# Issuing layer A of a two-layer trunk in the source's order

## Chip, core and metric

The kernel runs on one core of one Trainium2 chip. The metric is the device time of one execution in microseconds (us); of several runs the median is given. The engines are named as in the profile: PE is TensorE (matrix products), ACT is ScalarE, DVE is VectorE, POOL is GpSimd, and SP is the engine that issues most of the transfers (DMAs).

## The reference

A trunk of two layers works on 256 tokens of width 2048. Layer A is a Mamba-2 mixer, layer B is sliding-window attention with 32 heads over 4 shared key/value heads. Each layer ends in a layer norm of `alpha * x + mixer(x)`. Cut to what matters:

```python
# layer A
zxbcdt = x @ w_in                      # 2048 -> z 4096, x 4096, B 1024, C 1024, dt 64
xbc = silu(causal_conv4(xbc) + conv_b)
dt = softplus(dt_raw + dt_bias);  a = -exp(a_log)
y = ssd(xs, dt, a, B, C) + xs * d_skip # 8 groups of 8 heads, chunks of 128
y = y * silu(z)
y = y * rsqrt(mean(y**2 over a group's 512 columns) + EPS) * norm_w
x = layernorm(alpha * x + y @ w_out)
# layer B
k, v = x @ kv_w + kv_b (rotary on k);  q, gate = x @ w_in
o = softmax_with_sink(q k^T, window 128) v * silu(gate)
x = layernorm(alpha * x + o @ w_out)
```

All tensors are float32.

## The kernel before

**Units.** All weights come as units of 128 x 2048 values (1 MB). A unit is loaded in two raw halves of 512 KB (tile `wr`, five buffers), and each half is split: ACT rounds it to a high part (`wh`, line 137), DVE subtracts to get the low part (`wl`, line 138). Every product is then three matmuls, high x high, high x low and low x high, summed in PSUM (`mac`, lines 234 to 236). `fill_units` keeps `AHEAD` = 2 units split ahead of the one in use, and `load_unit` starts a unit's two transfers just ahead of its splits. High and low parts have four buffers each. The source list `srcs` holds the units in the order of use.

**Groups.** Layer A goes through eight groups of four 64-wide head pairs. A group has ten input blocks: B, C, four x blocks and four z blocks (group 0 takes z first). A block is one unit and 48 matmuls of 256 columns into one of four `mm` tiles in PSUM (`gemm_ws`). B, C and x blocks then pass a convolution and a silu (`conv_silu`: ACT line 402, three DVE steps line 404, ACT tanh line 407, DVE line 408); z blocks pass `in_z`. Spread among a group's blocks stand the four output units of the group before (`out_units`, `OUT_AT`): 24 matmuls of 512 columns each, in two halves, each followed by one DVE step (line 302) that adds the product, scaled by the group's rms, to the residual `xr`.

**The steps of a group.** The table `plan` says behind which block each further step stands; step t means block t % 10 of group t // 10. `load_decay` and `load_low` fetch the decay rows from DRAM, `sum_decay` and `exp_decay` (ACT) make the decay matrix `e`, `cb` multiplies B with C on PE and the result into `e` on DVE (lines 481 to 487), `tr` (group 0, on PE) or `turn_blocks`, `load_turned` and `scale_x` (other groups, by DVE and DRAM) turn x into `xd`, `ymm` multiplies `xd` with `e` (line 550), `gate` multiplies by silu(z), squares, and splits the result into `yH` and `yL` (POOL lines 566 to 572, ACT line 580, DVE line 581), and `norm` sums the squares on PE and takes an inverse root by three Newton rounds of four POOL instructions (lines 600 to 603).

**The opening.** Three first blocks run together, chunk by chunk as x and weights arrive (`load_first`, nine chunks in `FIRST`). The 64 delta columns are multiplied along with them, chunk by chunk (line 182), and `make_dt` turns them into step sizes and cumulated decays: ACT and DVE instructions in a chain that ends in a scan (line 368), a store to DRAM (`rscr`) and a PE transpose (`turn_dt`, line 378).

**What sets the order.** The source is traced, and a planner then orders each engine's instructions by priority and by its own estimate of when inputs are ready. `make_dt` stands under the highest priority, and parts of the z and convolution steps are raised too. Semaphores are set by the tool that places the tiles.

**After layer A.** `out_last` multiplies the last group's units, half 0 of the tokens first, with the layer norm's statistics (line 737) behind each. `done1` (lines 754 to 773) normalizes, transposes on PE (line 767) and splits x for layer B, whose first products (lines 809 to 811) give keys and values.

Of the kernel before, what the change touches and what calls it, by code (L numbers as in the profile page):

```python
# [15 lines left out]
P = 128  # L16
# [9 lines left out]
AHEAD = 2  # L26

TD, TS, CB0 = 6, 6, 9
# [3 lines left out]
NZERO = 3  # L32
XK_AT = (12, 13)
# [27 lines left out]
def trunk(ctx: ExitStack, tc: tile.TileContext, A: dict, out: bass.AP, dbg=None):  # L61
# [62 lines left out]
    def load_unit(src, places):  # L124
        u = new_unit(places)
        raws = []
        for c in range(2):
            raw = wp.tile([P, 1024], F32, tag="wr", name=nm("wr"), bufs=NR)
            nc.sync.dma_start(raw[:], src[:, c * 1024 : (c + 1) * 1024])
            raws.append(raw)  # L130
        for c in range(2):
            for (h, k0, k1), (l, _, _) in zip(*u.parts):
                a, b = max(k0, 8 * c), min(k1, 8 * c + 8)
                if a < b:
                    sl = slice((a - k0) * P, (b - k0) * P)
                    raw = raws[c][:, (a - 8 * c) * P : (b - 8 * c) * P]
                    nc.scalar.activation(h[:, sl], raw, AF.Copy)  # L137
                    nc.vector.tensor_tensor(l[:, sl], raw, h[:, sl].bitcast(F32), ALU.subtract)  # L138
        return u
# [25 lines left out]
    def products_first():  # L165

        zs = cc[:, :384]
        nc.vector.memset(zs, 0.0)
        junk = ax_tile()
        for i in range(NZERO):  # L170
            nc.tensor.matmul(junk[:, :S], zs[:, :P], zs[:, P:], start=True, stop=True)
        us, raws = load_first()
        units.extend(us)
        used[0] = NFIRST
        nc.sync.dma_start(pc[:], A["pc"])
        fill_units()
        pss = [mm_tile() for _ in us]
        pd = ax_tile()
        for (k0, k1), raw in zip(FIRST, raws):
            for k in range(k0, k1):  # L180
                rows = slice(64 * (k % 2), 64 * (k % 2) + 64)
                nc.tensor.matmul(
                    pd[rows, :S], raw[:, k - k0, FCOL - NHD :], raw[:, k - k0, :S], start=k < 2, stop=k >= KT - 2
                )
            for ps, u in zip(pss, us):
# [6 lines left out]
        return pd, pss  # L192
# [15 lines left out]
    for what, j in B_ORDER:  # L208
        if what == "g":
            broken.update(range(len(srcs), len(srcs) + 4))  # L210
        srcs += wo_srcs({"q": "wq", "g": "wg", "o": "wb"}[what], j)
    units = []
    used = [0]

    def fill_units():
        while len(units) < min(used[0] + AHEAD, len(srcs)):
            n = len(units)
            if n == 4:
                nc.sync.dma_start(cc[:], A["cc"])
# [6 lines left out]
            units.append(load_unit(srcs[n], BROKEN if n in broken else [WHOLE, WHOLE]))  # L226

    def next_unit():
        used[0] += 1
        fill_units()  # L230
        return units[used[0] - 1]
# [104 lines left out]
    def make_dt(ps):  # L336
        f = [ap.tile([P, S], F32, tag="sm", name=nm("f"), bufs=NSM) for _ in range(3)]
        f4 = ap.tile([P, 4, S], F32, tag="xs", name=nm("f4"), bufs=1)
        u, e, rec, z = [f4[:, i, :] for i in range(4)]
        w, q, dt = [x[:] for x in f]  # L340
        nc.scalar.copy(e, ps[:, :S])
        both = ax_tile()
        nc.tensor.matmul(both[:, :S], fold, e, start=True, stop=True)
        nc.scalar.activation(u, both[:, :S], AF.Identity, bias=pc[:, PC_DTB : PC_DTB + 1])
        nc.scalar.activation(e, u, AF.Abs)
        nc.scalar.activation(e, e, AF.Exp, scale=-1.0)
        aneg = ap.tile([P, 1], F32, tag="aneg", name="aneg")
        nc.scalar.activation(aneg[:], pc[:, PC_ALOG : PC_ALOG + 1], AF.Exp)
        nc.vector.tensor_scalar(aneg[:], aneg[:], -1.0, None, ALU.mult)
        nc.vector.tensor_scalar(rec, e, 2.0, None, ALU.add)  # L350
        nc.vector.reciprocal(rec, rec)
        nc.vector.tensor_tensor(z, e, rec, ALU.mult)
        nc.vector.tensor_tensor(w, z, z, ALU.mult)
        nc.vector.tensor_scalar(q, w, 1.0 / 15.0, None, ALU.mult)
        nc.vector.tensor_scalar(z, z, 2.0, None, ALU.mult)
        for d in (13.0, 11.0, 9.0, 7.0, 5.0, 3.0):
            nc.vector.scalar_tensor_tensor(q, q, 1.0 / d, w, ALU.add, ALU.mult)
        nc.vector.scalar_tensor_tensor(q, q, 1.0, z, ALU.add, ALU.mult)
        nc.vector.scalar_tensor_tensor(dt, u, 0.0, q, ALU.max, ALU.add)
        da, hi = e, rec  # L360
        nc.vector.tensor_scalar(da, dt, aneg[:], None, ALU.mult)
        nc.vector.tensor_scalar(hi, da, QUANT, None, ALU.add)
        nc.vector.tensor_scalar(hi, hi, QUANT, None, ALU.subtract)
        nc.vector.tensor_tensor(hi[64:128], da[64:128], hi[64:128], ALU.subtract)
        one = z
        nc.gpsimd.memset(one, 1.0)
        rc = w
        nc.vector.tensor_tensor_scan(rc, one, hi, 0.0, ALU.mult, ALU.add)
        nc.sync.dma_start(rscr[0:64, :], rc[:64])

        nc.scalar.activation(hi[64:128], rc[64:128], AF.Exp)
        nc.sync.dma_start(rscr[64:128, :], hi[64:128])
        return rc, dt, q
# [21 lines left out]
    def conv_silu(ps, t, dst):  # L395
# [5 lines left out]
        with tc.high_priority(CPRI):  # L401
            nc.scalar.activation(a[:], ps[:, :S], AF.Identity, scale=w(3), bias=w(4))  # L402
            for sft in (1, 2, 3):
                nc.vector.scalar_tensor_tensor(  # L404
                    a[:, sft:], ps[:, : S - sft], w(3 - sft), a[:, sft:], ALU.mult, ALU.add
                )
        nc.scalar.activation(dst, a[:], AF.Tanh)
        nc.vector.scalar_tensor_tensor(dst, dst, 1.0, a[:], ALU.add, ALU.mult)
# [61 lines left out]
    def in_z(g, i, ps):  # L470
        z = ap.tile([P, S], F32, tag="zz", name=nm("z"), bufs=4)
        with tc.high_priority(ZPRI):
            nc.scalar.activation(z[:], ps[:, :S], AF.Tanh, scale=0.5)
            nc.vector.scalar_tensor_tensor(z[:], z[:], 1.0, ps[:, :S], ALU.add, ALU.mult)
        gs[g].__dict__.setdefault("z", {})[i] = z

    def cb(g):
        st = gs[g]
# [30 lines left out]
    def turn_blocks(g):  # L509

        st = gs[g]
# [51 lines left out]
    def gate(g, i):  # L563
        st = gs[g]
        v = st.yz[:, i, :]
        nc.gpsimd.tensor_tensor(v, v, st.z[i][:], ALU.mult)  # L566
        q = ap.tile([P, S], F32, tag="sm", name=nm("sq"), bufs=NSM)
        nc.gpsimd.tensor_tensor(q[:], v, v, ALU.mult)
        if i == 0:
            st.ss = q  # L570
        else:
            nc.gpsimd.tensor_tensor(st.ss[:], st.ss[:], q[:], ALU.add)
        if i == 0:
            st.y = (
                yp.tile([P, 4, S], F32R, tag="yH", name=nm("yH"), bufs=2),
                yp.tile([P, 4, S], F32R, tag="yL", name=nm("yL"), bufs=2),
            )
        yH, yL = st.y
        c = PC_NW + g * 4 + i
        nc.scalar.activation(yH[:, i, :], v, AF.Copy, scale=pc[:, c : c + 1])  # L580
        nc.vector.scalar_tensor_tensor(
            yL[:, i, :], v, pc[:, c : c + 1], yH[:, i, :].bitcast(F32), ALU.mult, ALU.subtract
        )

    def norm(g):
# [13 lines left out]
        for _ in range(3):  # L599
            nc.gpsimd.tensor_tensor(t, r, r, ALU.mult)  # L600
            nc.gpsimd.tensor_tensor(t, t, v, ALU.mult)
            nc.gpsimd.tensor_scalar(t, t, -0.5, 1.5, ALU.mult, ALU.add)
            nc.gpsimd.tensor_tensor(r, r, t, ALU.mult)  # L603
        st.rms = r

    def group(g):
# [16 lines left out]
        if g == NG - 1:  # L623
            out_units(g - 1, [1])
            out_units(g - 1, [2, 3])
# [12 lines left out]
    dt_ps, first_ps = products_first()  # L638

    for c0, c1 in ((PC_CONV, PC_CONV + 240), (PC_NW, PC_NW + 32)):  # L640
        nc.vector.tensor_scalar(pc[:, c0:c1], pc[:, c0:c1], 0.5, None, ALU.mult)

    with tc.high_priority():
        dts = make_dt(dt_ps)
        load_decay(0, 0)

# [3 lines left out]

    def rotary():
        posi = ap.tile([P, 2], I32, tag="posi", name="posi")
        tc.keep_in_program_order(nc.gpsimd.dma_start(posi[:], A["pos"]))
        inv = ap.tile([P, 8], F32, tag="inv", name="inv")
        tc.keep_in_program_order(nc.gpsimd.dma_start(inv[:], A["inv"]))
# [33 lines left out]
    at(35, rotary)  # L689
    for g in range(NG):  # L690
        t = 10 * g
        if g == 0:
            at(TD, turn_dt, *dts)
            at(TS, load_decay, 0, 1)
            at(TS, load_low, 0)
            steps = TS
            pos = dict(cb=CB0, tr=12, y=13, norm=16)
# [24 lines left out]
        for i in range(4):  # L722
            at(t + pos["y"], gate, g, i)
# [436 lines left out]
```

## Time and profile before

| what | value |
|---|---|
| runs shown | 1001.55 us median of three (1000.96 to 1002.27) |
| the profiled execution | 1000.52 us, of which 998.7 from its first to its last instruction |
| PE busy | 984.9 us (99%) |
| DVE busy | 776.9 us (78%) |
| ACT busy | 533.7 us (53%) |
| POOL busy | 202.6 us (20%) |
| mean transfer rate | 219 GB/s, 218.72 MB |

A row of the busy times by stretch gives the stretch in us from the start, its length, then for each engine the busy time and in brackets the number of instructions, the share of its clock that PE was granted, the share of the transfer engines in use and their rate. A row of a group of instructions gives line, engine, operation, the tile written and the tiles read, shape and count, then busy us and the mean ns of one, then the idle time of the engine ahead of them with what ended it. A row of a timeline gives start, length, engine, line and operation, and in brackets the idle time ahead of it. A row of waits gives who waited for whom, us in total, times, the longest. [...]

### The profile page before, as it was taken

The page shows a single profiled execution, that of the slowest core. Times are in us where ns is not written, and L with a number is a line of the kernel's source. Part 1 is how long each engine was busy: PE and PEld are TensorE (multiplying, and loading weights), DVE is VectorE, ACT ScalarE, POOL GpSimd, SP SyncE. Part 2 cuts the span into 40 slices and gives each one's busy share as a digit, 9 for nine tenths or more (in the row PEclk, how much of TensorE's full clock was granted, in tenths as well). Part 3 has the DMA queues.
Part 4 walks back from the last instruction along what each step waited for, and adds up shares of the span by engine and source line. Part 5 has one row for each costly group of instructions (what it writes and reads, how often), then busy time and mean ns, then how long its engine had stood idle before and what let it go on. Part 6 is the DMA issues. An engine that isn't in the chain of part 4 may idle for free.

```text
span 998.7 us, 17607 instructions
## 1 busy us (share of the span) xinstructions
PE 984.9 (99%) x6836; PEld 880.7 (88%) x6836; DVE 776.9 (78%) x1147; ACT 533.7 (53%) x901; POOL 202.6 (20%) x321
## 2 busy tenths in 40 slices
PE   9999989999999999999999999999999999999997
PEld 7999979999998999999999999877898878777975
DVE  6769986786897697787788688889657586888786
ACT  6686736545645645644754654444355446444632
POOL 0000323203055120320320311320211303030202
PEclk9999999999999999999999999999999999999998
DMA  9697676686767657648658467555774848484942
GB/s 357 234 298 235 198 242 222 185 258 189 228 193 252 207 181 264 202 158 295 199 163 283 144 222 244 203 190 180 229 246 138 295 149 315 145 302 144 326 159 85
DMA packets 69444, 218.72 MB, mean 219 GB/s; under 512 B 8096, under 2 KB 19632, under 8 KB 68592
## 3 DMA queue, kind: packets, MB, share of 16 engines
q1 hardware_dynamic: 63648, 198.95, 60.9%
q0 software_dynamic: 5424, 18.12, 5.3%
q8 instruction: 54, 0.88, 0.3%
q10 hardware_dynamic: 288, 0.52, 0.1%
q14 instruction: 30, 0.25, 0.1%
HBM read 205.37 MB, written 12.19 MB: 218 GB/s over the span
## 4 chain that ended last, share of the span: by engine, by line
PE 82%; DVE 9%; DMA 4%; ACT 2%; issue 2%; POOL 1%; SPq 0%; DVEq 0%; POOLq 0%; ACTq 0%
PE mm L234 15%; PE mm L235 15%; PE mm L236 15%; PE mm L295 8%; PE mm L296 7%; PE mm L297 7%; PE mm L809 3%; PE mm L811 3%; PE mm L810 3%; DVE wl L138 2%; PE ax L550 2%; PE ax L922 1%; DMA wr<-in_wa 1%; PE ax L980 1%; DVE cv L404 1%
## 5 line engine op out<-in xcount | busy, mean ns | idle before, releaser
L138 DVE TENSOR_TENSOR wl<-wr,wh 128x1024 fp32r<-128x1024 f32 (+2 forms) x338 | 392.9, 1178 | 104.3 <-ACT wh L137 103.5
L137 ACT ACTIVATE wh<-wr 128x1024 fp32r<-128x1024 f32 (+2 forms) x338 | 334.9, 1012 | 201.4 <-PE mm L235 68.1
L234 PE MATMUL mm<-xH,wh 128*128 128x256 f32 x1280 | 355.7, 278 | 0.2 <-ACT wh L161 0.2
L235 PE MATMUL mm<-xL,wh 128*128 128x256 f32 x1280 | 354.5, 277 | 0.0
L236 PE MATMUL mm<-xH,wl 128*128 128x256 f32 x1280 | 354.3, 277 | 0.1
L234 PEld LDWEIGHTS mm<-xH,wh 128*128 128x128 f32 x1280 | 240.4, 188 | 5.0 <-ACT wh L161 2.2
L235 PEld LDWEIGHTS mm<-xL,wh 128*128 128x128 f32 x1280 | 240.4, 188 | 1.2 <-DVE xL L157 0.2
L236 PEld LDWEIGHTS mm<-xH,wl 128*128 128x128 f32 x1280 | 240.3, 188 | 0.4 <-DVE wl L138 0.3
L295 PE MATMUL mm<-wh,yH 128*128 128x512 f32 x256 | 102.0, 399 | 3.5 <-DVE xr L302 3.5
L296 PE MATMUL mm<-wh,yL 128*128 128x512 f32 x256 | 100.6, 393 | 0.0
L297 PE MATMUL mm<-wl,yH 128*128 128x512 f32 x256 | 100.4, 392 | 0.0
L566 POOL TENSOR_TENSOR yz<-yz,z 128x256 f32<-128x256 f32 x32 | 32.7, 1029 | 267.7 <-DVE yz L561 267.7
L404 DVE SCALAR_TENSOR_TENSOR cv<-mm,pc,cv 128x255 f32<-128x255 f32 x144 | 68.5, 476 | 8.9 <-ACT cv L402 7.6
L235 PE MATMUL mm<-x1L,wh 128*128 128x256 f32 x256 | 70.8, 277 | 0.0
L234 PE MATMUL mm<-x1H,wh 128*128 128x256 f32 x256 | 70.8, 276 | 0.0
L236 PE MATMUL mm<-x1H,wl 128*128 128x256 f32 x256 | 70.7, 276 | 0.0
L809 PE MATMUL mm<-wh,x1H 128*128 128x512 f32 x160 | 63.8, 399 | 0.0
L811 PE MATMUL mm<-wl,x1H 128*128 128x512 f32 x160 | 62.7, 392 | 0.5 <-DVE wl L138 0.4
L810 PE MATMUL mm<-wh,x1L 128*128 128x512 f32 x160 | 62.7, 392 | 0.2 <-DVE x1L L773 0.2
L295 PEld LDWEIGHTS mm<-wh,yH 128*128 128x128 f32 x256 | 48.4, 189 | 14.7 <-DVE xr L302 3.4
L302 DVE SCALAR_TENSOR_TENSOR xr<-mm,r,xr 128x512 f32<-128x512 f32 x64 | 46.1, 743 | 16.0 <-POOL r L603 10.0
L297 PEld LDWEIGHTS mm<-wl,yH 128*128 128x128 f32 x256 | 48.5, 189 | 10.3
(214 smaller groups left out, 1378.8 us busy)
## 6 DMA issues: line engine op xcount, KB each, us to landing
wr<-in_wa SPq DMA_DIRECT2D x154, 512.0 KB, 5.2
wr<-in_wo SPq DMA_DIRECT2D x64, 512.0 KB, 4.8
wr<-in_wq SPq DMA_DIRECT2D x32, 512.0 KB, 4.8
wr<-in_wg SPq DMA_DIRECT2D x32, 512.0 KB, 5.0
wr<-in_wb SPq DMA_DIRECT2D x32, 512.0 KB, 5.3
rb<-rscr SPq DMA_DIRECT2D x16, 512.0 KB, 5.3
el<-rscr SPq DMA_DIRECT2D x16, 256.0 KB, 4.9
wr<-in_wkv SPq DMA_DIRECT2D x8, 512.0 KB, 5.9
```

The lines of the kernel that those rows point to most:

```text
L137: nc.scalar.activation(h[:, sl], raw, AF.Copy)
L138: nc.vector.tensor_tensor(l[:, sl], raw, h[:, sl].bitcast(F32), ALU.subtract)
L234: nc.tensor.matmul(ps, ah, bh, start=first, stop=False)
L235: nc.tensor.matmul(ps, ah, bl, start=False, stop=False)
L236: nc.tensor.matmul(ps, al, bh, start=False, stop=last)
L295: nc.tensor.matmul(ps[:], aH[:, k, hs], u.h[:, ks], start=k == 0, stop=False)
L296: nc.tensor.matmul(ps[:], aL[:, k, hs], u.h[:, ks], start=False, stop=False)
L297: nc.tensor.matmul(ps[:], aH[:, k, hs], u.l[:, ks], start=False, stop=k == 3)
L404: nc.vector.scalar_tensor_tensor(a[:, sft:], ps[:, : S - sft], w(3 - sft), a[:, sft:], ALU.mult, ALU.add)
L809: nc.tensor.matmul(ps[:], x1H[:, kk, hs], u.h[:, ks], start=kk == 0, stop=False)
L810: nc.tensor.matmul(ps[:], x1L[:, kk, hs], u.h[:, ks], start=False, stop=False)
L811: nc.tensor.matmul(ps[:], x1H[:, kk, hs], u.l[:, ks], start=False, stop=kk == KT - 1)
```

## The change

Up to the end of layer A's groups the five engines issue in the order of the source (`manual_schedule`), and the source is laid out anew so that each engine's order is meant. First norm and layer B stay with the planner.

- **Order.** The region covers the opening and all eight groups. The raised priorities go.
- **Transfers.** Raw halves are now requested by `load_half`, one behind each split, five ahead.
- **Units ahead.** One unit is split ahead in the opening, two from the end of the opening on, three from unit 16 on; two again for the rest after layer A.
- **Put off.** The second part of a convolution (tanh and last DVE step) waits in `posts` until the next unit has been split (`flush`).
- **Delta chain.** `make_dt` becomes a class in pieces: `copy` and `fold` inside the opening's products, `begin` behind them, `end` behind block 3, `turn` behind block 5 (`TD` 6 to 5). The delta products of the chunks are taken in five visits (`DT_VISITS`) instead of eight.
- **Group 0.** `tr` and `ymm` move from steps 12 and 13 to 10 and 11.
- **Gate.** First the four products, then the squares and sums; the split into `yH` and `yL` becomes a step of its own (`split_y`), two steps later. In the last group it stands between the third and the fourth output unit of the group before.
- **Norm.** The Newton rounds move from POOL (four instructions each) to DVE (three each).
- **Rotary.** Its two small loads move to step 33, its arithmetic from step 35 to 36.

```diff
-AHEAD = 2
-TD, TS, CB0 = 6, 6, 9
+AHEAD = 3
+MORE_AT = 16
+TD, TS, CB0 = 5, 6, 9
+DT_VISITS = {0: (0, 1), 2: (2,), 3: (3, 4), 5: (5, 6), 6: (7, 8)}
...
+    def load_half():
+        if halves:
+            n, c = halves.pop(0)
+            raws[n, c] = raw = wp.tile([P, 1024], F32, tag="wr", name=nm("wr"), bufs=NR)
+            nc.sync.dma_start(raw[:], srcs[n][:, c * 1024 : (c + 1) * 1024])
...
                     nc.scalar.activation(h[:, sl], raw, AF.Copy)
                     nc.vector.tensor_tensor(l[:, sl], raw, h[:, sl].bitcast(F32), ALU.subtract)
+            load_half()
...
+        for _ in range(2):
+            load_half()
+        nc.sync.dma_start(cc[:], A["cc"])
+        load_half()
         fill_units()
+        dts = DT()
...
+        for i, (k0, k1) in enumerate(FIRST):
+            for j in DT_VISITS.get(i, ()):
+                ...
+            if i == 0:
+                for _ in range(2):
+                    load_half()
+            if i == 6:
+                dts.copy(pd)
+            for j, (ps, u) in enumerate(zip(pss, us)):
+                if i == 7 and j == 2:
+                    dts.fold()
...
+        dts.begin()
+        ahead[0] = 2
...
     def fill_units():
-        while len(units) < min(used[0] + AHEAD, len(srcs)):
+        while len(units) < min(used[0] + ahead[0], len(srcs)):
             n = len(units)
-            if n == 4:
-                nc.sync.dma_start(cc[:], A["cc"])
+            if n == MORE_AT:
+                ahead[0] = AHEAD
...
     def next_unit():
         used[0] += 1
         fill_units()
+        flush()
...
-        with tc.high_priority(CPRI):
-            (ACT start and three DVE steps of the convolution)
-        nc.scalar.activation(dst, a[:], AF.Tanh)
-        nc.vector.scalar_tensor_tensor(dst, dst, 1.0, a[:], ALU.add, ALU.mult)
+        (the same, without priority)
+        def rest():
+            nc.scalar.activation(dst, a[:], AF.Tanh)
+            nc.vector.scalar_tensor_tensor(dst, dst, 1.0, a[:], ALU.add, ALU.mult)
+        posts.append(rest)
...
+            def store():
+                nc.scalar.activation(hi[64:128], rc[64:128], AF.Exp)
+                nc.sync.dma_start(rscr[64:128, :], hi[64:128])
+                load_decay(0, 0)
+            posts.append(store)
...
-    def gate(g, i):
+    def gate(g):
+        for i in range(4):
+            nc.gpsimd.tensor_tensor(v, v, st.z[i][:], ALU.mult)
+        for i in range(4):
+            (square on POOL, and from the second on the sum)
+    def split_y(g):
+        for i in range(4):
+            (yH on ACT, yL on DVE)
...
         for _ in range(3):
-            nc.gpsimd.tensor_tensor(t, r, r, ALU.mult)
-            nc.gpsimd.tensor_tensor(t, t, v, ALU.mult)
-            nc.gpsimd.tensor_scalar(t, t, -0.5, 1.5, ALU.mult, ALU.add)
-            nc.gpsimd.tensor_tensor(r, r, t, ALU.mult)
+            nc.vector.scalar_tensor_tensor(t, r, -0.5, r, ALU.mult, ALU.mult)
+            nc.vector.tensor_tensor(t, t, v, ALU.mult)
+            nc.vector.scalar_tensor_tensor(r, t, 1.5, r, ALU.add, ALU.mult)
...
-            out_units(g - 1, [2, 3])
+            out_units(g - 1, [2])
+            for fn, *a in plan.pop(10 * g + 11):
+                fn(*a)
+            out_units(g - 1, [3])
...
+    order.enter_context(tc.manual_schedule(engines={E.PE, E.DVE, E.Activation, E.Pool, E.SP}))
+    dts, first_ps = products_first()
...
-            pos = dict(cb=CB0, tr=12, y=13, norm=16)
+            pos = dict(cb=CB0, tr=10, y=11, norm=16)
...
+        at(t + pos["y"] + 2, split_y, g)
...
     for g in range(NG):
         group(g)
+    order.close()
     w_stack.close()
+    ahead[0] = 2
```

More of the change, by code (lines that the diff above doesn't have):

```diff
@@ L122, in new_unit, with load_unit @@
         return u
-    def load_unit(src, places):
+    raws = {}
+    def load_half():
[3 more added lines that the diff above has]
+            nc.sync.dma_start(raw[:], srcs[n][:, c * 1024 : (c + 1) * 1024])
+    def load_unit(n, places):
         u = new_unit(places)
-        raws = []
         for c in range(2):
[L128 to L131, printed above, removed]
+            half = raws.pop((n, c))
             for (h, k0, k1), (l, _, _) in zip(*u.parts):
@@ L334, in trunk @@
     rscr = dram.tile([P, S], F32, tag="rscr", name="rscr")
[L336 to L373, printed above, removed]
@@ new lines, in trunk, with __init__, copy, fold @@
+    class DT:
+        def __init__(self):
+            f = [ap.tile([P, S], F32, tag="sm", name=nm("f"), bufs=NSM) for _ in range(3)]
+            f4 = ap.tile([P, 4, S], F32, tag="xs", name=nm("f4"), bufs=1)
+            self.u, self.e, self.rec, self.z = [f4[:, i, :] for i in range(4)]
+            self.w, self.q, self.dt = [x[:] for x in f]
+            self.aneg = ap.tile([P, 1], F32, tag="aneg", name="aneg")
+            nc.scalar.activation(self.aneg[:], pc[:, PC_ALOG : PC_ALOG + 1], AF.Exp)
+            nc.vector.tensor_scalar(self.aneg[:], self.aneg[:], -1.0, None, ALU.mult)
+        def copy(self, ps):
+            nc.scalar.copy(self.e, ps[:, :S])
+        def fold(self):
+            self.both = ax_tile()
+            nc.tensor.matmul(self.both[:, :S], fold, self.e, start=True, stop=True)
+        def begin(self):
+            u, e, rec, z, w, q = self.u, self.e, self.rec, self.z, self.w, self.q
+            nc.scalar.activation(u, self.both[:, :S], AF.Identity, bias=pc[:, PC_DTB : PC_DTB + 1])
+            nc.scalar.activation(e, u, AF.Abs)
+            nc.scalar.activation(e, e, AF.Exp, scale=-1.0)
+            nc.vector.tensor_scalar(rec, e, 2.0, None, ALU.add)
+            nc.vector.reciprocal(rec, rec)
+            nc.vector.tensor_tensor(z, e, rec, ALU.mult)
+            nc.vector.tensor_tensor(w, z, z, ALU.mult)
+            nc.vector.tensor_scalar(q, w, 1.0 / 15.0, None, ALU.mult)
+            nc.vector.tensor_scalar(z, z, 2.0, None, ALU.mult)
+        def end(self):
+            u, e, rec, z, w, q, dt = self.u, self.e, self.rec, self.z, self.w, self.q, self.dt
+            for d in (13.0, 11.0, 9.0, 7.0, 5.0, 3.0):
+                nc.vector.scalar_tensor_tensor(q, q, 1.0 / d, w, ALU.add, ALU.mult)
+            nc.vector.scalar_tensor_tensor(q, q, 1.0, z, ALU.add, ALU.mult)
+            nc.vector.scalar_tensor_tensor(dt, u, 0.0, q, ALU.max, ALU.add)
+            da, hi = e, rec
+            nc.vector.tensor_scalar(da, dt, self.aneg[:], None, ALU.mult)
+            nc.vector.tensor_scalar(hi, da, QUANT, None, ALU.add)
+            nc.vector.tensor_scalar(hi, hi, QUANT, None, ALU.subtract)
+            nc.vector.tensor_tensor(hi[64:128], da[64:128], hi[64:128], ALU.subtract)
+            one = z
+            nc.gpsimd.memset(one, 1.0)
+            rc = w
+            nc.vector.tensor_tensor_scan(rc, one, hi, 0.0, ALU.mult, ALU.add)
+            nc.sync.dma_start(rscr[0:64, :], rc[:64])
+            def store():
[3 more added lines that the diff above has]
+            posts.append(store)
+        def turn(self):
+            turn_dt(self.w, self.dt, self.q)
```

116 lines of the change are left out of this document (64 added, 52 removed).

## The prediction

> **What bounds the kernel now.** I read the page's totals first, then the chain of work that ended last, then the busy times by stretch, with limits set where that chain changes its character.
>
> ```profile
> span 998.7 us, 17607 instructions
> ## 1 busy us (share of the span) xinstructions
> PE 984.9 (99%) x6836; PEld 880.7 (88%) x6836; DVE 776.9 (78%) x1147; ACT 533.7 (53%) x901; POOL 202.6 (20%) x321
> ```
>
> ```profile
> 152.65 2.75 PE ax L550 x32
> ...
> 188.76 0.54 PE ax L481 x2
> ```
>
> ```profile
> core 0: us, PE busy (x) PEld busy (x) DVE busy (x) ACT busy (x) POOL busy (x), PEclk, DMA share, GB/s
> 17.67:20.50 2.83, 2.83 (x23) 2.32 (x23) 2.83 (x9) 2.44 (x8) 0.00 (x0) 1.00 0.99 345
> 87.42:97.26 9.84, 9.46 (x90) 8.20 (x88) 9.58 (x18) 6.90 (x10) 0.00 (x0) 1.00 0.87 312
> 125.80:136.11 10.31, 7.35 (x27) 5.61 (x25) 7.46 (x8) 3.45 (x4) 4.11 (x12) 0.83 0.46 150
> 152.65:233.23 80.58, 80.58 (x618) 75.85 (x620) 63.20 (x84) 44.23 (x67) 15.64 (x23) 1.00 0.70 218
> 160.90:188.26 27.36, 27.36 (x241) 27.35 (x240) 19.38 (x26) 18.23 (x28) 5.57 (x6) 1.00 0.67 208
> 205.75:211.21 5.46, 5.46 (x27) 4.51 (x25) 4.85 (x9) 2.59 (x4) 0.00 (x0) 1.00 0.94 271
> 644.36:689.12 44.76, 42.34 (x197) 32.87 (x195) 40.72 (x59) 17.23 (x23) 5.78 (x15) 1.00 0.53 182
> 655.52:691.24 35.72, 33.30 (x154) 25.38 (x153) 35.37 (x51) 13.71 (x20) 1.65 (x3) 1.00 0.39 124
> 700.00:800.00 100.00, 100.00 (x653) 88.80 (x652) 60.95 (x104) 49.13 (x96) 20.74 (x33) 1.00 0.70 225
> ```
>
> The busy share of TensorE (99%) overstates it, since neighbouring matmuls overlap; the pace of the stretches is what counts. 160.90 to 188.26 is five input blocks: 240 matmuls in 27.36 us, 0.114 us each, 5.47 a block. An output unit (24 matmuls of 512 columns) takes 5.46. At that pace a full group takes 80.58, with no idle: groups 2 to 6 and layer B (700 to 800, 100.00 busy) are TensorE's own, and no order can shorten them. Whatever the change brings lies ahead of 152.65 and around the first norm.
>
> ```profile
> PE mm L295 <- DVE xr L302: 3.0, 1, 3.0
> PE ax L171 <- DVE cc L168: 1.3, 1, 1.3
> PE ax L378 <- DVE f L368: 0.9, 1, 0.9
> PE ax L550 <- DVE xd L502: 0.3, 1, 0.3
> ```
>
> These are TensorE's waits up to 160 us, in us. The large one is the output units of group 0, which the timelines show:
>
> ```profile
> 128.31 0.39 PE L297 MATMUL mm<-wl,yH 128*128 128x512 f32 x1
> 131.66 0.50 PE L295 MATMUL mm<-wh,yH 128*128 128x512 f32 x1 [2.96 <-DVE xr L302]
> ```
>
> ```profile
> 130.62 0.19 POOL L603 TENSOR_TENSOR r<-r 128x2 f32<-128x2 f32 x1
> ```
>
> VectorE's update of the residual (L302) needs the group's rms, whose twelve Newton steps on POOL ended at 130.81, as the last of them shows; all four matmul tiles of PSUM were full by then. The unit took 10.31 us instead of 5.46: 4.85 lost, about 3 of it idle and 1.9 at a lower clock (0.83 in that row).
>
> **The change, part by part.** The prices of one piece, in ns the second number of each row; silu and z updates are pieces of 256 columns like L502's, about 0.4 us, on either engine:
>
> ```profile
> L138 DVE TENSOR_TENSOR wl<-wr,wh 128x1024 fp32r<-128x1024 f32 x46 | 55.5, 1224 | 5.6 <-ACT wh L137 5.5
> L404 DVE SCALAR_TENSOR_TENSOR cv<-mm,pc,cv 128x255 f32<-128x255 f32 (+2 forms) x36 | 17.1, 476 | 8.0 <-ACT cv L402 7.6
> L486 DVE TENSOR_TENSOR e<-e,cbm 128x1536 f32<-128x1536 f32 x4 | 6.9, 1747 | 0.0
> ...
> L302 DVE SCALAR_TENSOR_TENSOR xr<-mm,r,xr 128x512 f32<-128x512 f32 x7 | 5.0, 741 | 2.9 <-POOL r L603 2.9
> ...
> L502 DVE TENSOR_TENSOR xd<-ax,dtx 128x256 f32<-128x256 f32 x4 | 1.6, 416 | 0.0
> L515 DVE STREAM_TRANSPOSE zt<-xs 128x512 f32<-128x512 f32 x2 | 1.3, 686 | 0.0
> ...
> L598 DVE TENSOR_SCALAR r<-r 128x2 int32<-128x2 int32 x1 | 0.2, 160 | 0.0
> ```
>
> ```profile
> L137 ACT ACTIVATE wh<-wr 128x1024 fp32r<-128x1024 f32 x46 | 48.0, 1056 | 34.4 <-DMA wr<-in_wa 13.6 <-DMA wr<-in_wo 9.4 <-DVE z L474 6.1
> L443 ACT ACTIVATE e<-rb,rtk 128x256 f32<-128x256 f32 (+1 forms) x40 | 14.5, 445 | 1.0 <-DMA rb<-rscr 1.0
> L402 ACT ACTIVATE cv<-mm,pc 128x256 f32<-128x256 f32 x12 | 6.6, 546 | 0.0
> L450 ACT ACTIVATE e<-e 128x1536 f32<-128x1536 f32 x4 | 5.9, 1475 | 0.0
> ```
>
> *Opening.* The delta products go from eight visits on TensorE to five. A step of 18 macs with a visit took 2.83, the macs alone 18 x 0.114 = 2.05, so a visit is 0.78 with its products. The products stay; only three changeovers go: between 0 and half of 3 x 0.78. I take -0.5. A visit to two chunks waits for the later of them; should that one land late, it adds up to a visit, 0.78.
>
> *Delta chain.* `fold` moves up into step 7, the chain's first half before the z blocks, its second half to block 3. Counted in the new order: `fold` is done near 26 (seven steps of 2.83), VectorE then has six pieces (4 us, an estimate, the reciprocal being longer), three z updates 1.2, the splits of units 4 and 5 4.9, a z update and thirteen pieces 5.6: the scan near 42. TensorE ends step 9 at 20.50 + 3 x 2.83 - 0.5 = 28.5 and block 5 three blocks later, 44.9, where `turn_dt` now stands. Its wait of 0.9 on L368 goes: -0.9 (0 if these 3 us of cover are used up). SP holds the broadcast of the decay rows until the scan's store has landed, and the raw halves queued behind it wait too; five halves, 2.5 units or 13.7 us, lie ahead of TensorE there: 0. Unit 4 is split after the first half and the three z updates; by my count its first low half is ready 1 us before TensorE wants it, and would cost that much if late.
>
> *`ymm` of group 0, two blocks earlier (11 for 13).* Before, 87.42 to 97.26 holds a block, the transposes and `ymm`: 9.84 - 5.47 - 2.75 = 1.62 for transposes and waits; I count 0.5 as wait, and it goes. The new place is tight. From the end of block 9 TensorE has `cb` 0.54, two blocks 10.94 and the transposes (about 0.8): 12.3 us. VectorE, now strictly in order, has the last convolution and its silu with two hand-overs to ScalarE (about 2.9), the mask product (0.5), two decay products (3.5), unit 12's splits (2.4), block 10's convolution (1.4) and xd (4 x 0.416 = 1.7): 12.4. On time that costs 0.1, but ScalarE comes late: blocks 6 to 8 give it sixteen decay pieces (7.1), two exponentials (1.475 each, 3.0) and three units' splits, tanh and convolution starts (3 x (2 x 1.056 + 0.4 + 0.55) = 9.2), 19.3 in 16.4 us of TensorE, so it is up to 3 behind, part of it caught up. I take +1.3; ends 0 and 4.5.
>
> *Norm on VectorE.* Twelve POOL steps become nine VectorE steps of about 0.2 (L598's 0.16 and the hand-over). The 4.85 us go. What is late next is VectorE itself. From the end of block 6 of group 1 (plan step 16) to the moment when TensorE needs back the tile of the first output half (four tiles on), TensorE has `cb` 0.54, a unit 5.46, a block 5.47, half a unit 2.73 and the norm's own products (an estimate, 0.4): 14.6. VectorE has ahead of that tile's update: block 5's rest (its convolution, two silus, the block transposes, and two hand-overs to ScalarE: 4.7), a unit's splits 2.4, z 0.4, norm 2.4, mask and decay 4.0, the next splits 2.4, the update 0.7: 17.0. So TensorE waits 2.4 there: net -4.85 + 2.4. Ends of the new wait: 0 (VectorE caught up before) and 5.5 (three more behind, as at `ymm`).
>
> A wait of 2.4 is taken at full clock; the one of 3.35 above brought it down. [...]
>
> *Gate and split.* POOL has the same eleven pieces, products first; the split into high and low follows two steps later, 10.9 us, and its first reader is three units after that: 0 (2 us on ScalarE and VectorE each if POOL were that late).
>
> *Groups 2 to 6.* SP, ScalarE and VectorE now hold their place behind each wait; behind a convolution's start, for example, stand the next splits, their transfers and the silu. Three units ahead from unit 16 cover two blocks, 10.9 us. VectorE has 63.2 busy of 80.58 and gains 1.8 from the norm; no wait at TensorE: 0. Without the cover, each microsecond counts once per group.
>
> *First norm.* In 655.52 to 691.24 VectorE is busy 35.37 of 35.72: here it is the bound. It started late:
>
> ```profile
> 650.23 0.16 DVE L598 TENSOR_SCALAR r<-r 128x2 int32<-128x2 int32 x1
> 651.42 2.36 DVE L138 TENSOR_TENSOR wl<-wr,wh 128x1024 fp32r<-128x1024 f32 x2 [1.03 <-ACT wh L137]
> 655.52 0.75 DVE L302 SCALAR_TENSOR_TENSOR xr<-mm,r,xr 128x512 f32<-128x512 f32 x1 [1.75 <-POOL r L603]
> ```
>
> With rms on VectorE the 1.75 and most of the 1.03 go; one unit more is already split (2.4 less), the nine steps add 1.8. That is about 3 us less VectorE time. TensorE's own work in 644.36 to 689.12 is 96 + 63 matmuls at 0.2275 (5.46/24) and 32 transposes, about 39 with changeovers 41: 44.76 can fall by 4 at most. I take -2.4; ends 0, since this stretch is still scheduled and may come out in another order, and -4.
>
> *Layer B and the tail.* Raw halves are requested five ahead as before: 0, plus or minus 1. The rotary loads move three blocks ahead of use and cost nothing.
>
> Sum: -0.5 - 0.9 - 0.5 + 1.3 - 4.85 + 2.4 - 2.4 = -5.45. The profiled execution took 1000.52 in all (span 998.7), so 995.1; the median of the runs shown is 1.03 above it, 1001.55, so **996.1**.
>
> **Rivals.** (A) *Slower: a wait in every group.* At steps 4 and 5 VectorE has convolution 1.4, norm 2.4, mask and decay 4.0, two units' splits 4.9, a silu 0.4 and the update 0.7, 13.8, before the tile that TensorE needs back after 17.4 (`cb` 0.54, norm 0.4, a unit, two blocks). The margin is 3.6. If VectorE enters step 4 more than 3.6 behind, TensorE waits in each of five groups; from 1.1 us a group the gain is gone, and 1.7 gives +3, 1004.6. For it: no engine can pass a late piece any more. Against it: 17 us of VectorE free in each group.
>
> (B) *The waits of the front only move.* `ymm` waits 4.5 and the units of group 0 wait 5 as before: -0.5 - 0.9 - 0.5 + 4.5 - 4.85 + 5 - 2.4 = +0.3, 1001.9, no change. For it: both margins above are near zero. With the lower clock behind such a wait, 1003.8.
>
> (C) *No new wait.* VectorE is not behind at either place, and the norm gives all: -0.5 - 0.9 - 0.5 - 4.85 - 4.0 = -10.75, 990.8.
>
> That the order is the old one under a new name is excluded: the rms changes engine, and `ymm` its block, whatever the rest does.
>
> **How the numbers follow.** The forecast with its own range 993 to 999.3 has 0.50, C 0.20, B 0.17, A 0.13. Faster by over 0.2% (about what a measurement of this kernel can tell from no change; 2 us) is the forecast, C and a little of B: 0.75. Within 0.2%: most of B, 0.13; slower: A and the lower clock, 0.12. The range 989.0 to 1002.5 leaves out the ends of C and most of A.
>
> **What would show it.** Right: no POOL piece between the norm's product and L302's successor; TensorE's first `ymm` near 81 with a wait of 1 to 2 on xd; a wait of 2 to 3 on the residual update in group 0's second output unit at full clock; the second `ymm` near 149 to 150 instead of 152.65; group period 80.6; the first norm's stretch 42 to 43 long. Wrong, if a group takes over 81, if the second `ymm` is after 152, or if the stretch after the last group's norm is as long as now.

## The result, and the profile after

The changed kernel takes 994.08 us in the median (993.42 to 995.80), the kernel before 1001.91 beside it (1000.96 to 1003.66): ratio 0.9922, 95% interval 0.9903 to 0.9942, 7.8 us less. The profiled execution took 993.8 us, span 992.0; before it was 1000.52 and 998.7. The page's totals after:

```profile
span 992.0 us, 17541 instructions
## 1 busy us (share of the span) xinstructions
PE 979.9 (99%) x6836; PEld 879.6 (89%) x6836; DVE 791.1 (80%) x1219; ACT 532.1 (54%) x901; POOL 171.2 (17%) x225
```

VectorE has 14.2 us more to do (the Newton steps alone are 72 more instructions), POOL 31.4 less. To see where the 6.7 us of the span went, both spans are cut at the same events: the start of the last product of the opening's three units, the first `cb`, group 0's norm, the second `ymm` (before: 152.58, the first of its matmuls), the last group's norm, the last transposes of the first norm. The busy times by stretch, before (the row 644.36:689.12 stands in the prediction) and after; columns as there:

```profile
0.00:29.26 29.26, 27.68 (x183) 21.43 (x184) 17.34 (x43) 17.79 (x45) 0.28 (x5) 1.00 0.90 342
29.26:69.99 40.73, 39.82 (x343) 39.25 (x342) 31.21 (x54) 29.93 (x50) 0.31 (x1) 1.00 0.77 254
69.99:113.78 43.79, 43.33 (x382) 41.81 (x381) 41.23 (x59) 30.55 (x52) 9.26 (x11) 1.00 0.74 238
113.78:152.58 38.80, 35.84 (x226) 32.02 (x225) 31.50 (x39) 18.73 (x23) 5.16 (x12) 0.96 0.72 240
152.58:644.36 491.78, 491.78 (x3754) 461.70 (x3754) 387.17 (x525) 270.34 (x404) 122.65 (x186) 1.00 0.67 212
...
689.12:998.70 309.58, 304.10 (x1764) 251.57 (x1762) 227.69 (x370) 149.09 (x311) 59.16 (x91) 0.99 0.64 213
```

```profile
0.00:28.30 28.30, 27.00 (x184) 22.03 (x185) 18.09 (x44) 18.62 (x46) 0.28 (x5) 1.00 0.93 355
28.30:67.71 39.41, 39.41 (x344) 39.00 (x342) 33.41 (x58) 28.55 (x48) 0.31 (x1) 1.00 0.70 216
67.71:111.00 43.29, 42.85 (x383) 41.85 (x382) 40.45 (x58) 31.80 (x52) 11.79 (x11) 1.00 0.81 270
111.00:147.35 36.35, 34.24 (x227) 30.84 (x225) 32.56 (x49) 17.37 (x21) 0.00 (x0) 1.00 0.84 274
147.35:639.12 491.77, 491.77 (x3753) 461.67 (x3753) 398.21 (x581) 269.57 (x404) 97.95 (x114) 1.00 0.67 213
639.12:682.03 42.91, 42.09 (x196) 32.93 (x195) 40.76 (x66) 17.25 (x23) 1.62 (x3) 1.00 0.55 187
682.03:992.00 309.97, 302.57 (x1764) 251.28 (x1762) 227.57 (x370) 148.99 (x311) 59.22 (x91) 1.00 0.64 213
```

The differences are -0.96, -1.32, -0.50, -2.45, -0.01, -1.85 and +0.39: -6.70. All of the gain lies ahead of the second `ymm` and in the first norm; from the second `ymm` to the last group's norm, six groups in a row, both kernels take 491.8 us. TensorE's waits after, those of 0.4 us and more up to the end of layer A:

```profile
PE mm L330 <- DVE xr L337: 2.1, 1, 2.1
PE ax L178 <- DVE cc L175: 1.3, 1, 1.3
...
PE ax L609 <- DVE xd L560: 0.4, 1, 0.4
```

The wait on the scan (L368) is gone, and the wait on the residual update, 3.0 before, is still there at 2.1. VectorE's timeline ahead of that update, after (start, us, instruction):

```profile
118.78 0.15 DVE L661 TENSOR_SCALAR r<-ax 128x2 f32<-128x2 f32 x1
...
120.94 0.16 DVE L668 SCALAR_TENSOR_TENSOR r<-r 128x2 f32<-128x2 f32 x1
121.02 0.55 DVE L541 TENSOR_TENSOR cbm<-ax,cc 128x384 f32<-128x384 f32 x1
121.61 3.42 DVE L544 TENSOR_TENSOR e<-e,cbm 128x1536 f32<-128x1536 f32 x2
124.95 2.35 DVE L144 TENSOR_TENSOR wl<-wr,wh 128x1024 fp32r<-128x1024 f32 x2
127.22 1.40 DVE L337 SCALAR_TENSOR_TENSOR xr<-mm,r,xr 128x512 f32<-128x512 f32 x2
```

There is no idle time in it: the norm is done at 121.1, and the update stands behind 3.9 us of mask and decay products and 2.3 of splits. It starts 16.2 us behind the norm's product (111.00), against 17.1 before (113.78 to 130.85). So the rms is not what the update waits for any more; it waits for its turn.

### The profile page after: what moved, and what is told of

Read it like the earlier page. It is cut to its first block, busy times and chain, and to the rows that moved or that the text cites. A ratio compares the mean times of both kernels' runs of the same rounds, so it can differ in the third digit from the quotient of the medians.

```text
span 992.0 us, 17541 instructions
## 1 busy us (share of the span) xinstructions
PE 979.9 (99%) x6836; PEld 879.6 (89%) x6836; DVE 791.1 (80%) x1219; ACT 532.1 (54%) x901; POOL 171.2 (17%) x225
## 5 line engine op out<-in xcount | busy, mean ns | idle before, releaser
L144 DVE TENSOR_TENSOR wl<-wr,wh 128x1024 fp32r<-128x1024 f32 (+2 forms) x338 | 398.0, 1207 | 94.9 <-ACT wh L143 94.2
L143 ACT ACTIVATE wh<-wr 128x1024 fp32r<-128x1024 f32 (+2 forms) x338 | 328.6, 1012 | 193.5 <-PE mm L331 68.8
L455 ACT ACTIVATE cv<-mm,pc 128x256 f32<-128x256 f32 x48 | 26.8, 559 | 62.4 <-PE mm L271 62.4
```

## The experiments

Two questions were open: is it the engine of the Newton rounds or the order that brings the gain, and what is the wait of 2.1 us made of? Times are medians; each ratio is to the kernel before on the same chip. "Front" below is the time from the opening's last product to the second `ymm`: 123.3 us before, 119.1 after.

**1. Newton back on POOL, in the pinned order.**

```diff
-            nc.vector.scalar_tensor_tensor(t, r, -0.5, r, ALU.mult, ALU.mult)
+            nc.gpsimd.tensor_tensor(t, r, r, ALU.mult)
...
```

> The changed kernel, with the three Newton rounds of the norm back on POOL (twelve small steps) and nothing else undone. Theory E (the engine, as the prediction had it): the residual update of group 0's second output unit waits for POOL again; idle time of TensorE there rises from 2.5 to 3.4 us or more, the granted clock drops in that unit as before the change, it takes about 10 us instead of 7.9, and the first norm's stretch is 1 to 2 us longer: 994.1 + 2.4 + 1.5 = about 998. Rival O (the order): in the changed kernel VectorE is busy up to the update at 127.2 us with mask, decay and split pieces; POOL can do its twelve steps beside them, VectorE is freed of nine steps of 0.2 us, and the update comes up to 1.8 us earlier: -1 to -1.8 at that unit, +1 to +2 at the first norm: 993 to 995, the same within 0.2%.

996.11 us (993.94 to 998.26), ratio 0.9938 (0.9921 to 0.9956). POOL's steps, then VectorE's update, and the stretch of the output unit:

```profile
121.30 1.66 POOL L668 TENSOR_SCALAR r<-r 128x2 f32<-128x2 f32 x1
123.04 1.59 POOL L669 TENSOR_TENSOR r<-r 128x2 f32<-128x2 f32 x1
124.71 1.05 POOL L666 TENSOR_TENSOR r<-r 128x2 f32<-128x2 f32 x1
...
126.99 0.19 POOL L668 TENSOR_SCALAR r<-r 128x2 f32<-128x2 f32 x1
```

```profile
128.59 1.41 DVE L337 SCALAR_TENSOR_TENSOR xr<-mm,r,xr 128x512 f32<-128x512 f32 x2 [1.75 <-POOL r L669]
```

```profile
124.31:133.83 9.52, 7.33 (x26) 5.56 (x25) 7.77 (x10) 3.40 (x5) 3.59 (x9) 0.82 0.91 342
```

VectorE, freed of nine steps, stands 1.75 us for POOL, and the update comes 16.3 us behind the norm's product, as with the rounds on VectorE (16.2). Neither theory holds whole: at this place the engine is worth nothing. In the first norm it is worth 0.8 (642.11 to 685.82, 43.71 us, against 42.91). What else the profiled run lost is 1.5 us in the opening (its last product at 29.85, against 28.30) and the clock, 0.82 in the row, after a wait of 2.2 us, hardly more than the changed kernel's 2.1 with the clock at 1.00.

**2. Newton on VectorE, in the planner's order.** The reverse edit in the kernel before.

> The kernel before, with only the norm's Newton rounds moved to VectorE (nine steps); the planner's order, the transfers and all else as before. Theory E: this alone takes most of the gain: VectorE no longer stands idle for 2.85 us before the update, the unit of 10.31 us takes 7 to 7.9 with the clock at full speed (-2.5 to -3.3), the first norm loses its wait of 1.75 us on POOL (-1 to -2): 1001.9 - 4.5 = about 997.5. Rival O: the planner finds other pieces to put ahead of the update; the unit stays above 9 us and the time within 0.2% of 1001.9.

1005.43 us, ratio 1.0025 (1.0010 to 1.0040): slower, which neither theory had. VectorE's timeline shows why:

```profile
124.67 0.17 DVE L598 TENSOR_SCALAR r<-r 128x2 int32<-128x2 int32 x1
124.74 1.76 DVE L486 TENSOR_TENSOR e<-e,cbm 128x1536 f32<-128x1536 f32 x1
126.41 0.16 DVE L600 SCALAR_TENSOR_TENSOR r<-r 128x2 f32<-128x2 f32 x1
126.48 1.76 DVE L486 TENSOR_TENSOR e<-e,cbm 128x1536 f32<-128x1536 f32 x1
128.15 0.16 DVE L601 TENSOR_TENSOR r<-r 128x2 f32<-128x2 f32 x1
128.22 1.22 DVE L138 TENSOR_TENSOR wl<-wr,wh 128x1024 fp32r<-128x1024 f32 x1
...
132.74 1.41 DVE L302 SCALAR_TENSOR_TENSOR xr<-mm,r,xr 128x512 f32<-128x512 f32 x2
```

The planner puts a long piece between each of the first small steps and the next, up to the fifth of the nine. From L598 to the last of them they take 8.0 us (in the change, L664 at 119.17 to 121.10, 1.9), the update comes 18.8 us behind the norm's product, and TensorE waits 4.7. The stretch from the second `ymm` to the last group's norm grows by 2.1 us (493.91), with a wait of 1.73 at 285.8; the first norm gains 0.8 (43.96 against 44.76). In this kernel, then, the move of the rounds costs more than it brings.

**3. The changed layout without the pinned order.**

```diff
-    order.enter_context(tc.manual_schedule(engines={E.PE, E.DVE, E.Activation, E.Pool, E.SP}))
```

> The changed kernel without the region of source order: layout, put-off second parts, transfer requests, places of the steps and the norm on VectorE as in the change, but the planner orders the engines in layer A. If the pinned order is what shortens the front (second ymm at 147.4 us instead of 152.6), the second ymm goes back to 150 or later and the time to 997 to 1000. If layout and norm do it, the time stays within 0.2% of 994.1. Full groups stay at 80.6 us each in both.

1002.34 us, ratio 1.0001 (0.9989 to 1.0013): the whole gain is gone. TensorE waits 4.42 us in the opening on a split of `x` (`xL`), 1.8 on the scan and 1.6 on the residual update; the second `ymm` starts at 156.83. Most of the loss stands in the opening, and has nothing to do with the norm: its last product starts at 34.40, against 28.30. The planner puts the rotary's arithmetic at the head of VectorE's queue, where it waits for its two small loads, and the first splits of `x` stand behind it (in the kernel before, also the planner's order, it ran at 283 us):

```profile
8.41 0.36 DVE L728 TENSOR_SCALAR ang<-inv,posf 128x8 f32<-128x8 f32 x2 [3.17 <-DMA inv<-in_inv]
...
9.95 0.42 DVE L164 TENSOR_TENSOR xL<-first,xH 128x256 fp32r<-128x256 f32 x1
```

```profile
10.42 0.58 PE L270 MATMUL mm<-xL,wh 128*128 128x256 f32 x1 [4.42 <-DVE xL L164]
```

The front behind it takes 122.4 us, against 119.1 in the change and 123.3 before. The Newton steps are spread as in run 2 (129.15 to 136.65, 7.5 us), yet the wait on the update is no longer than in the change. The first norm keeps its 42.88 us: this part of the gain does not need the pinned order. The layout was written for a fixed order and the raised priorities are gone, so this shows what the pair is worth, not what the planner could make of a layout of its own.

**4. `cb` of group 1 behind the update.**

```diff
-            pos = dict(cb=6, zt=ZT_AT, ld=LD_AT, xd=XD_AT, y=Y_AT, norm=10 + CB_AT)
+            pos = dict(cb=7, zt=ZT_AT, ld=LD_AT, xd=XD_AT, y=Y_AT, norm=10 + CB_AT)
```

> The changed kernel with the cb step of group 1 (mask product and the two decay products on VectorE, 4.1 us together) one block later, at plan step 17 instead of 16, so behind the residual update that group 0's second output unit waits for. Theory: TensorE's idle 2.5 us in that unit is VectorE's queue and nothing else; the update comes about 4 us earlier and the unit takes 5.5 us instead of 7.9: 994.1 - 2.4 = 991.7. Rival: the queue of VectorE is only moved; the wait turns up again at the next reader of a late piece (the next block's split weights, or the second ymm at step 19), and the second ymm still starts at 147.4: 994.1.

991.19 us, ratio 0.9890 (0.9873 to 0.9907). The update, and the unit's stretch:

```profile
122.33 1.40 DVE L337 SCALAR_TENSOR_TENSOR xr<-mm,r,xr 128x512 f32<-128x512 f32 x2
```

```profile
122.31:127.87 5.56, 5.56 (x27) 4.60 (x26) 3.92 (x6) 2.35 (x3) 0.00 (x0) 1.00 1.03 382
```

12.0 us behind the norm's product instead of 16.2, the unit at TensorE's pace, and no wait of TensorE from the opening to the second `ymm` (front 116.2). The wait was VectorE's queue and nothing else.

**5. The same edit in the kernel before.**

> The kernel before, with only the cb step of group 1 (mask product and two decay products on VectorE) placed at plan step 17 instead of 16; Newton rounds on POOL and the planner's order as before. Theory: the decay products hold up both VectorE and POOL (POOL's steps took 1.6 us beside them instead of 0.2); behind the update they hold up neither, the second output unit of group 0 takes 5.5 to 7 us instead of 10.3 at full clock, and the time is 1002.4 - 4 = about 998.5. Rival: the planner puts other long pieces between the norm's steps, as it did with the rounds on VectorE, and the unit stays above 9 us: within 0.2% of 1002.4.

999.70 us, ratio 0.9979 (0.9964 to 0.9993): the theory's way, by 2.5 us instead of 4. The unit took 6.64 us at full clock, but TensorE waited 2.4 on the scan and 1.2 on `xd`, where it had waited 0.9 and 0.3. POOL's twelve steps, still on POOL, took 3.2 us (127.60 to 130.83), 0.19 to 0.20 each, instead of 6.1: what had held them up were the decay products, beside which two of them had taken 1.63 and 1.59.

**6. Newton on POOL with `cb` at 17.** Edits 1 and 4 together.

> The changed kernel with cb of group 1 at step 17 and the Newton rounds back on POOL. With the rounds on POOL and cb at 16, POOL's twelve steps took 7.8 us (1.6 each beside the decay products, 1.05 beside the splits, 0.2 alone) and VectorE waited 1.75 us for them. [...] Rival: POOL's steps are slow whatever stands beside them; the unit takes 8 us or more: 994 or slower.

993.03 us, ratio 0.9903 (0.9882 to 0.9924). The unit took 5.56 us, against the rival's 8 or more. POOL's steps, the first, third and last:

```profile
118.81 1.11 POOL L666 TENSOR_TENSOR r<-r 128x2 f32<-128x2 f32 x1 [20.10 <-DVE r L664]
...
121.15 0.19 POOL L668 TENSOR_SCALAR r<-r 128x2 f32<-128x2 f32 x1
...
123.62 0.20 POOL L669 TENSOR_TENSOR r<-r 128x2 f32<-128x2 f32 x1
```

5.0 us for the twelve instead of 7.8: the first two stand beside two splits, the rest run at 0.2. In the front the engine costs nothing (116.2, as in run 4); in the first norm it cost 2.0 here (44.90 us), more than the 0.8 of run 1.

**7. `tr` and `ymm` of group 0 one block later** (steps 11 and 12).

> The changed kernel with group 0's tr and ymm one block later (steps 11 and 12 instead of 10 and 11; its split with them). Theory: VectorE is the queue that sets the front, and its work up to the residual update of group 0's second output unit is the same; TensorE no longer idles 0.5 us ahead of the first ymm, and idles that much longer in the output unit (2.6 to 3.2 instead of 2.5), so 994 to 994.6, and up to 1.7 more where the clock drops there. Rival: the two waits are independent of each other; the first goes, the second stays at 2.5: 993.5.

992.74 us, ratio 0.9907 (0.9892 to 0.9922), not to be told from the change (its interval overlaps). The wait ahead of `ymm` went, the other did not grow (1.93 us): the rival is nearer. The front is 0.9 us longer than in the change (119.9), the opening of this profile 1.3 shorter, by the scatter that the next section describes. The clock dropped in the unit all the same:

```profile
121.22:130.28 9.06, 7.13 (x27) 5.41 (x26) 9.06 (x10) 3.45 (x4) 0.00 (x0) 0.84 0.95 322
```

**8. Two units ahead throughout** (`AHEAD = 2`).

> The changed kernel with two units split ahead throughout, never three. Theory: VectorE has 64 us of work in 80.58, so two units of cover are enough in the full groups: period 80.58, the front unchanged up to the second ymm; the first norm's stretch loses the unit that was split before it and takes 44 instead of 42.9: 995. Rival: in a strict order two blocks of cover are too few for the steps with 13 us of VectorE work; TensorE waits in each full group, 1 us or more each: 1000 or slower.

998.96 us, ratio 0.9965 (0.9953 to 0.9976). The full groups stayed at 80.58 us, as the theory had it, but the place of the loss was another: the front became 2 us shorter, the first norm 7.3 longer. Its stretch, and the row of VectorE that explains it:

```profile
636.25:686.47 50.22, 45.16 (x197) 34.99 (x195) 42.72 (x68) 17.20 (x23) 1.62 (x3) 0.93 0.54 179
```

```profile
645.24 1.23 DVE L144 TENSOR_TENSOR wl<-wr,wh 128x1024 fp32r<-128x1024 f32 x1 [4.51 <-ACT wh L143]
```

Here the last group's Newton steps have splits between them, and one of these stood 4.51 us for ScalarE; TensorE waited 3.6 us on the residual update and the clock was 0.93 in the row. The third unit costs in the front and pays before the first norm.

**9. The third unit only from unit 40 on** (`MORE_AT = 40`).

> The changed kernel with the third unit split ahead only from unit 40 on instead of unit 16. Theory: with two units ahead throughout, group 0's second output unit took 6.4 us instead of 7.9 and the first ymm-to-ymm stretch was 2 us shorter, because VectorE has one unit's splits (2.4 us) less ahead of the residual update; what that kernel lost, it lost at the first norm (50 us instead of 42.9). So here the front gains 1.5 to 2 and the first norm stays at 42.9: 994.1 - 2 = 992. Rival: the shorter unit there was chance (the update needed both anyway), and the time stays at 994.

991.41 us, ratio 0.9896 (0.9881 to 0.9912), as the theory had it: the unit took 6.45 us, the first norm 42.90.

**10. `cb` at 17 and the third unit from unit 40 on.**

> The changed kernel with cb of group 1 at step 17 and the third unit only from unit 40 on. Theory: with cb at 17 TensorE has no wait left between the first products and the second ymm, so nothing is left to gain there: 991, the same as with cb at 17 alone. Rival: the two edits add up, 989.

990.02 us, ratio 0.9879 (0.9865 to 0.9894), the fastest here, 1.2% under the kernel before. Its interval overlaps that of `cb` at 17 alone, and the front is the same (116.3 against 116.2), so the second edit's share is not shown.

**11. The split of `y` directly behind the gate.**

```diff
...
-        at(t + pos["y"] + 2, split_y, g)
+        at(t + pos["y"], split_y, g)
```

> The changed kernel with the split of the gated rows (ScalarE and VectorE, four pieces each) directly behind the gate in the same step, instead of two steps later. Now ScalarE and VectorE, in strict order, stand 4 to 5 us behind POOL's four products (1.06 us each) in every group. Theory: with three units split ahead (16 us) that is hidden in groups 2 to 6 (period 80.58), but not in the front, where VectorE is without slack between 80 and 127 us: idle time in group 0's second output unit grows from 2.5 to 5 us or more with a drop of the clock, 997 to 1000. Rival A: hidden everywhere, 994. Rival B: a wait in each full group, above 1002.

999.67 us, ratio 0.9969 (0.9952 to 0.9987). The output unit of group 0, and a full group:

```profile
124.30:136.75 12.45, 8.19 (x27) 6.20 (x26) 12.38 (x14) 3.58 (x5) 0.00 (x0) 0.74 0.95 325
475.96:556.54 80.58, 80.58 (x617) 75.84 (x616) 64.82 (x93) 44.25 (x66) 9.26 (x11) 1.00 0.67 214
```

As the theory had it: hidden in the full groups, 5.9 us dearer in the front (wait 4.3, clock 0.74).

**12. Copy and fold of the delta products behind the opening.**

```diff
-            if i == 6:
-                dts.copy(pd)
...
+        dts.copy(pd)
+        dts.fold()
         dts.begin()
```

> The changed kernel with the copy and the fold of the delta products behind all products of the opening instead of within step 7, some 2.8 us later; the turn stays behind block 5. Theory (the prediction's step): the scan comes at 44.6 instead of 41.8 us, the turn at 44.9 waits 0.3 to 0.9 us for it, and VectorE, 85% busy between 29 and 74 us, has caught up by the first ymm: 994.1 + 0.3 to 0.9. Rival: VectorE has no slack left before group 0's second output unit; the wait of 2.5 us there grows to about 5 and the clock drops: 998 or slower.

997.41 us, ratio 0.9954 (0.9938 to 0.9970): neither expectation held. `turn_dt` does not wait. VectorE stands longer ahead of the chain (6.14 us, 2.92 in the change), and the splits queued behind the chain come late:

```profile
29.82 0.29 DVE L393 TENSOR_SCALAR f<-f 128x256 f32<-128x256 f32 x1 [6.14 <-ACT f L392]
```

```profile
35.53 0.39 PE L269 MATMUL mm<-xH,wl 128*128 128x256 f32 x1 [1.23 <-DVE wl L144]
```

The front is 4.0 us longer than in the change. Some 1.7 come from there (starts 1.51, 0.27, 0.22 and 0.19 us apart around 34, where 0.114 is the pace), 0.2 are the fold's two products, which now stand behind the opening. The update's wait stayed at 2.2, but the clock fell to 0.82 in that unit, which took 9.55 us, 1.7 more.

## Why the prediction was right, point by point

Forecast 996.1 (995.1 against the profiled execution), measured 994.1 (993.8): the gain came where it was put, in the front and the first norm, and the sum is 1.3 short.

- *Opening*: predicted -0.5, measured -0.96. The profiles scatter here: the first 18 macs took 2.28 to 4.08 us, part of them started 0.21 us apart instead of 0.114. (A matmul of 256 columns is 0.28 long in the rows, so neighbours overlap, and the pace is that of the starts.) In the change's trace the wide starts stand at 6.27, 6.49, 6.70 and 6.92, and from 7.08 to 8.46 the starts are 0.11 to 0.13 apart. Its records of the granted clock begin at 6.99; a row counts what lies ahead of the first record as 1.00, so the rows do not show what the clock was there. The last product started between 27.0 and 29.9 in ten profiles of pinned kernels (28.7 at most but for one), at 29.3 to 29.4 in three of the order before.
- *Delta chain*: predicted -0.9, measured -1.32. The scan ran at 41.75 (predicted near 42), the turn at 44.85 (44.9) with no wait. Run 12 adds what the prediction did not count: the earlier chain also keeps the splits behind it on time.
- *`ymm`*: predicted -0.5 + 1.3, measured -0.50. This is the term that was mis-sized: the new wait on `xd` is 0.4. I took ScalarE as up to 3 us late and charged 1.3; it was not: ahead of this `ymm` it stood 2.5 and 3.9 us itself, for VectorE's convolutions.
- *Norm*: predicted -4.85 + 2.4 = -2.45, measured -2.45 (38.80 to 36.35), with a wait of 2.1 at full clock in the unit predicted. The size is right and half of the reason is wrong. The count of VectorE's pieces (17.0 ahead of the update against 14.6 of TensorE) was the right picture, and run 4 shows it; that the twelve POOL steps were what had to go was not, as runs 1 and 6 show. Of the 2.45, 0.86 is the shorter wait (3.35 to 2.49 between the two starts), the other 1.6 the clock that did not fall. That a wait of 2.4 passes at full clock was my assumption: no run shows a length up to which the clock holds. The wait of 2.1 had 1.00 in its unit, those of 1.93 to 2.2 in runs 7, 1 and 12 had 0.82 to 0.84 (see the last section), so the full clock here was luck.
- *First norm*: predicted -2.4, measured -1.85, 42.91 long (42 to 43 was the sign). Runs 1 and 2 give 0.8 for the rms on VectorE (run 6 gave 2.0), which leaves some 1.05 for the layout; run 3 shows that the pinned order has no part in it. Run 8 points to the unit split ahead, but its clock loss stands on top.
- *Groups 2 to 6, gate and split*: 0, as measured. Run 11 shows that `split_y`'s two steps are needed in the front and not in these groups; run 8 that two units cover them.
- *Layer B and the tail*: 0 plus or minus 1, measured +0.39.

Of the signs, two were off: the wait on `xd` (1 to 2; it is 0.4) and the second `ymm` (149 to 150; it is 147.35), from the first three terms. Rival A's margin of 3.6 us in each group was never used up in any pinned kernel. Rival B fell because the wait at `ymm` is small. Rival C, no new wait, is what run 4 makes of the kernel: 991.2, against its 990.8. That the numbers meet is partly chance, since C took 4.0 from the first norm, which gave 1.9.

## What to carry to other kernels

Keep a short chain of dependent small steps together where it releases a long one: it took 1.9 us in the pinned order, 7.5 to 8.0 where the planner spread it between long pieces. What the spread costs depends on the queue around it: TensorE waited 4.7 us on the update in run 2, 1.6 in run 3. Before an operation is moved to another engine, count what stands in the queue ahead of its reader; here the reader's own queue was the bound, and one long step put behind it gained 2.9 us, the move of the norm in the same pinned order nothing in the front. A planner that is free to move small steps can also move them ahead of what a kernel needs first, as run 3 shows. Look-ahead is not free in strict order: each unit split early stands ahead of something, so let its depth grow only where the front is past.

## What the runs showed of the hardware

The clock fell after shorter idle times than the 2.4 us that I had taken for safe. TensorE's timeline in run 7 shows the wait, and the first slow matmul 1.26 us behind it:

```profile
126.05 0.50 PE L330 MATMUL mm<-wh,yH 128*128 128x512 f32 x1 [1.93 <-DVE xr L337]
...
127.31 0.60 PE L332 MATMUL mm<-wl,yH 128*128 128x512 f32 x1
```

The change's wait at the same place, in its own timeline, left the clock at 1.00:

```profile
128.02 0.50 PE L330 MATMUL mm<-wh,yH 128*128 128x512 f32 x1 [2.10 <-DVE xr L337]
```

The waits on the residual update in group 0's second output unit, and the granted clock in that unit's row:

| kernel | wait, us | clock |
|---|---|---|
| run 3 | 1.6 | 1.00 |
| run 7 | 1.93 | 0.84 |
| the change | 2.10 | 1.00 |
| run 1 | 2.2 | 0.82 |
| run 12 | 2.2 | 0.82 |
| the kernel before | 2.96 | 0.83 |
| run 11 | 4.3 | 0.74 |
| run 2 | 4.7 | 0.74 |

The change's wait was longer than run 7's and left the clock at 1.00, so the length of the wait alone does not decide; what else does is not shown.

In run 1 a step of 128 x 2 on POOL took 0.19 to 0.20 us while VectorE stood waiting (126.99 to 128.55), 1.66 and 1.59 beside VectorE's two decay products (both in 3.43, from 121.15), 1.05 and 1.06 beside its two splits (both in 2.35, from 124.49). The mask product (0.55 from 120.56) also reads two tiles, and the step beside it, at 120.73, took 0.20. What a piece of VectorE must be to stretch a step on POOL is not shown beyond these.
